# Masked softmax on one core: VectorE by half tiles, the first tile stored whole, and two later starts for GpSimd's narrow loads

## The chip, the core and the metric

The kernel runs on one core of a Trainium2 chip. The metric is device time in microseconds of one execution; smaller is better. Inputs and output lie in the chip's memory (HBM), and the kernel moves them through the core's on-chip memory (SBUF, 128 partitions).

## The reference

```python
def setup_inputs():
    batch, heads, seq_q, seq_k = 16, 8, 256, 256
    return {
        "x": np.random.randn(batch, heads, seq_q, seq_k).astype(np.float32),
        "lengths": np.random.randint(seq_k // 2, seq_k, size=batch).astype(np.int32),
    }

def reference(x, lengths):
    result = np.zeros_like(x)
    for b in range(batch):
        length = lengths[b]
        masked = x[b, :, :, :length].copy()
        masked = masked - np.max(masked, axis=-1, keepdims=True)
        exp_masked = np.exp(masked)
        result[b, :, :, :length] = exp_masked / np.sum(exp_masked, axis=-1, keepdims=True)
    return result
```

Each of the 16 batches has a length of its own between 128 and 255: a softmax over the first `length` of 256 columns, zeros behind them. The lengths of this draw are 188, 233, 229, 243, 195, 252, 165, 210, 222, 180, 209, 157, 159, 199, 214 and 248.

## The kernel before

One batch is one tile: 2048 rows of 256 numbers, as 128 partitions of 16 rows, 16 KB in each partition and 2 MB in all. SBUF holds eight such slots (`xt`), and the tile at position n lies in slot n % 8. Positions 0 to 2 are batches 1 to 3, position 3 is batch 0, and from 4 on position and batch agree (`batch_of`). In the text "tile n", "load n", "mask n" go by position, and "a" and "b" are the first and second eight rows of each partition (the halves).

Each tile goes through five steps, on four engines that run by themselves and wait for each other by semaphores only:

- **Load.** SyncE issues the loads of tiles 0 (two halves), 1 and 2 in full width at the start (L136, L138). GpSimd issues those of tiles 3 to 15 (`pick`, L158): it reads the batch's length and branches to a load of the smallest fitting width from a list, so that fewer bytes are read. The columns right of 160 in slots 3 to 7 have been zeroed before (L180). The first narrow load (tile 3) waits until the first half of tile 0 has been exponentiated (`s_exp` 1, L183), the second (tile 4) until two halves have been divided (`s_out` 2, L186). In the loop, each further load waits for the load two before it to have landed (L192, L196) and for its slot's last tile to have been stored (L193).
- **Mask**, on VectorE (`clip`, L234): in columns 128 to 255 it takes the minimum of x and a steep ramp that is very large left of `length` and very negative from there on, so that the exponential gives zero. Tile 0 by halves, all others whole. It counts `s_min`.
- **Exponential**, on ScalarE (L341): sixteen activations per tile, eight per half, each of which also sums its row. After each half it counts `s_exp`. The loop waits for the mask of the tile (`s_min` i // 2 + 2).
- **Divide**, on VectorE: reciprocal of eight sums (L255) and a product over one half (L258). It counts `s_out`, two per tile.
- **Store.** SyncE issues all stores on one queue (L147), in the order of the tiles: tile 0 in two halves, 1 to 7 as a half and two quarters, 8 to 12 and 15 in halves, 13 and 14 whole (`parts`). Each waits for its divide (L144), and the first one of a tile for the store of the tile two before it to have landed (L146). Ahead of the first store SyncE waits for three masks (`s_min` 3, L140), which is when the mask of tile 1 is done.

VectorE's order is written out by hand (L265 to L277): both half masks of tile 0, then for each tile divide a, the whole mask of the next tile, divide b; for tile 1 the mask of tile 2 comes ahead of both divides. After the last tile VectorE and TensorE look whether any sum was out of bounds, and a slower second pass, not taken with these inputs, would then run.

SyncE's transfers run on queue q1 of the profile, GpSimd's on q0. Both feed the same 16 transfer engines.

Of the kernel before, what the change touches and what calls it, by code (L numbers as in the profile page):

```python
# [16 lines left out]
ACT = mybir.EngineType.Activation  # L17
# [4 lines left out]
def kernel(  # L22
# [6 lines left out]
    nc = tc.nc  # L29
    P = nc.NUM_PARTITIONS  # L30

    batch, heads, seq_q, seq_k = x.shape
    rows = heads * seq_q
    assert rows % P == 0
    nt = rows // P
    half = nt // 2
# [8 lines left out]
    ahead = 3  # L45
# [11 lines left out]
    def parts(b):  # L57


        if b == 0:  # L60
            cuts = [0, half, nt]
        elif b < 8:
            cuts = [0, half, half + quarter, nt]
        elif b < 13 or b == batch - 1:
            cuts = [0, half, nt]
        else:
            cuts = [0, nt]
        return [slice(i, j) for i, j in zip(cuts, cuts[1:])]
# [30 lines left out]
    with tc.tile_critical(no_gpsimd_drain=True):  # L99
# [11 lines left out]
        s_min = sem("s_min")  # L111
        s_exp = sem("s_exp")
        s_out = sem("s_out")
# [10 lines left out]
        def length(engine, at):  # L124

            return nc.values_load(
                at,
                engines=[engine],
                skip_runtime_bounds_check_because="compared with constants, never an address",
            )  # L130
# [6 lines left out]
        for b in range(1, ahead):  # L137
            nc.sync.dma_start(out=xt[:, b], in_=x_f[batch_of(b)]).then_inc(s_ld[b + 1], 16)  # L138

        nc.sync.wait_ge(s_min, 3)  # L140
        for b in range(batch):
            s_b = s_st[b % 2]
            for s in parts(b):
                nc.sync.wait_ge(s_out, 2 * b + (s.stop - 1) // half + 1)  # L144
                if b >= 2 and s.start == 0:
                    nc.sync.wait_ge(s_b, 64 * (b // 2 + 1))  # L146
                nc.sync.dma_start(  # L147
                    out=out_f[batch_of(b), :, s, :], in_=xt[:, b % slots, s, :]
                ).then_inc(s_b, 16 * ((s.stop - s.start) // quarter))
# [1 line left out]

        def pick(v, b, slot, par, ws):

            if len(ws) == 1:
                w = ws[0]
                nc.gpsimd.dma_start(  # L158
                    out=xt[:, slot, :, :w], in_=x_n[:, b, :, :w]
                ).then_inc(s_sw[par], 16)  # L160
                return
            m = (len(ws) - 1) // 2
            with nc.gpsimd.If(v <= ws[m]):  # L163
                pick(v, b, slot, par, ws[: m + 1])
            with nc.gpsimd.Else():
                pick(v, b, slot, par, ws[m + 1 :])

        x_n = x_f.rearrange("b p t c -> p b t c")
        x_g = x_f.rearrange("b p t c -> p b (t c)")
# [10 lines left out]
            nc.gpsimd.memset(xt[:, b, :, low:], 0.0).then_inc(s_fill, 1)  # L180
        nc.gpsimd.wait_ge(s_word, 16)
        nc.gpsimd.wait_ge(s_fill, slots - ahead)
        nc.gpsimd.wait_ge(s_exp, 1)  # L183
        v_len = length(POOL, word[0:1, 0:1])
        pick(v_len, 0, ahead, 1, [160, 176, 192, 208, 224, seq_k])
        nc.gpsimd.wait_ge(s_out, 2)  # L186
        with nc.Fori(0, batch // 2 - 2, 1, engines=[POOL]) as q:
            for par in range(2):
                n = 2 * q + (ahead + 1 + par)
                v_len = length(POOL, word[0:1, bass.ds(2 * n, 1)])  # L190
                with nc.gpsimd.If(q >= 1):
                    nc.gpsimd.wait_ge(s_sw[par], 16 * q + 16 * par)  # L192
                    nc.gpsimd.wait_ge(s_st[par], 64 * q)  # L193
                if par:
                    with nc.gpsimd.Else():
                        nc.gpsimd.wait_ge(s_sw[par], 16)  # L196
                pick(v_len, bass.ds(n, 1), bass.ds(n % slots, 1), par, widths + [seq_k])
# [9 lines left out]
        v = 0  # L207

        def step(ins):
            nonlocal v  # L210
            v += 1
            ins.then_inc(s_v, 1)
# [18 lines left out]
        def clip(b, s, lo, hi):  # L231

            t = xt[:, b % slots, s, lo:hi]
            return nc.vector.scalar_tensor_tensor(  # L234
                out=t,
                in0=down[:, None, lo:hi].to_broadcast([P, s.stop - s.start, hi - lo]),
                scalar=len_s[:, batch_of(b) : batch_of(b) + 1],
                in1=t,
                op0=ALU.add,
                op1=ALU.min,  # L240
            )

        def mask(b, s):
            if b == 0:
                nc.vector.wait_ge(s_ld[s.start // half], 16)
            elif b < ahead:
                nc.vector.wait_ge(s_ld[b + 1], 16)
            else:
                nc.vector.wait_ge(s_sw[b % 2], 16 * ((b - 1) // 2))
            clip(b, s, mid, seq_k).then_inc(s_min, 1)  # L250

        def divide(b, h):
            s = slice(h * half, (h + 1) * half)
            nc.vector.wait_ge(s_exp, 2 * b + h + 1)
            step(nc.vector.reciprocal(out=inv_sum[:, b, s], in_=row_sum[:, b, s]))  # L255
            nc.vector.wait_ge(s_v, v)
            t = xt[:, b % slots, s, :]
            nc.vector.tensor_tensor(  # L258
                out=t,
                in0=t,  # L260
                in1=inv_sum[:, b, s, None].to_broadcast([P, half, seq_k]),
                op=ALU.mult,
            ).then_inc(s_out, 1)

        mask(0, slice(0, half))  # L265
        mask(0, slice(half, nt))
        for b in range(batch):


            first = b != 1  # L270
            if first:
                divide(b, 0)
            if b + 1 < batch:
                mask(b + 1, slice(0, nt))
            if not first:
                divide(b, 0)
            divide(b, 1)  # L277

# [56 lines left out]
        def rows(at, i):  # L337

            for j in range(half):
                e = x_h[:, at, j, :]  # L340
                ins = nc.scalar.activation(out=e, in_=e, func=EXP, accum_out=sum_h[:, i, j])  # L341
            ins.then_inc(s_exp, 1)


        nc.scalar.wait_ge(s_min, 1)
        rows(slice(0, 1), slice(0, 1))
        with nc.Fori(1, 2 * batch, 1, engines=[ACT]) as i:  # L347
            nc.scalar.wait_ge(s_min, i // 2 + 2)
            rows(bass.ds(i % (2 * slots), 1), bass.ds(i, 1))

        nc.scalar.wait_ge(s_redo, 1)
# [53 lines left out]
```

## Time and profile before

| | |
|---|---|
| median of 3 runs | 155.42 us (155.26 to 155.69) |
| the profiled execution | 155.72 us, its span 154.1 us |
| bytes moved | 61.57 MB (HBM read 27.98, written 33.55) |
| VectorE busy | 116.9 us (76%) |
| ScalarE busy | 105.3 us (68%) |
| GpSimd busy | 21.5 us (14%) |
| q1 (SyncE): bytes, share of the 16 engines | 39.85 MB, 62.6% |
| q0 (GpSimd): bytes, share | 21.69 MB, 35.4% |
| half divide (L258) | 2292 ns, 32 times |
| whole mask (L234), half mask | 2.35 us, 1.28 us |

The profile shows one execution. Its span begins and ends inside that execution, so the time of the run is 1.6 us longer. The page cuts the span into 40 slices of 3.85 us and gives for each the busy tenths of an engine, the mean busy share of the 16 transfer engines, and the GB/s that they moved. A row of a timeline has start, duration, engine, line and operation, and in brackets the idle time ahead of it and what ended that.

### The profile page before, as it was taken

What the parts mean: (1) busy time and instruction counts of PE and PEld (TensorE: products, weight loads), DVE (VectorE), ACT (ScalarE), POOL (GpSimd) and SP (SyncE); (2) the same over time, 40 slices, a digit from 0 to 9 for tenths busy, and PEclk for the clock granted to TensorE, in tenths of its full rate; (3) what the DMA queues carried; (4) which work ended last, traced back from release to release, by engine and by line L of the source; (5) the groups of instructions that cost most, each with busy time, mean ns of one, the idle gap of its engine ahead of it and who ended that gap; (6) DMA issues with size and microseconds to landing.
All of it is one profiled execution on the core that took longest, in us unless ns stands there. A gap on an engine that the chain in (4) does not pass through costs nothing.

```text
span 154.1 us, 1305 instructions
## 1 busy us (share of the span) xinstructions
PE 0.3 (0%) x2; PEld 0.2 (0%) x2; DVE 116.9 (76%) x91; ACT 105.3 (68%) x514; POOL 21.5 (14%) x28
## 2 busy tenths in 40 slices
PE   0000000000000000000000000000000000000000
PEld 0000000000000000000000000000000000000000
DVE  1349899969889696969697896969696566977800
ACT  3096899587795959595968859595959609688000
POOL 4953020100220200202020020202010000000000
DMA  4999999999999999999999999999999999999992
GB/s 115 421 451 417 327 372 417 419 409 441 417 401 391 418 416 422 405 414 418 395 426 406 413 412 404 415 420 414 419 420 413 432 437 413 430 442 430 425 419 106
DMA packets 10357, 61.57 MB, mean 400 GB/s; under 512 B 866, under 2 KB 978, under 8 KB 6642
## 3 DMA queue, kind: packets, MB, share of 16 engines
q1 hardware_dynamic: 5904, 39.85, 62.6%
q0 software_dynamic: 4448, 21.69, 35.4%
q14 instruction: 3, 0.02, 0.0%
q10 hardware_dynamic: 2, 0.00, 0.0%
HBM read 27.98 MB, written 33.55 MB: 399 GB/s over the span
## 4 chain that ended last, share of the span: by engine, by line
DMA 67%; DVE 16%; ACT 4%; issue 4%; SPq 2%; ACTq 1%; POOLq 0%; PE 0%
DMA out_dram<-xt 34%; DMA xt<-in_x_dram 33%; DVE xt L258 9%; DVE xt L234 6%; ACT xt L341 4%; SPq L147 1%; ACTq L341 1%; DVE inv_sum L255 1%; SPq L136 1%; DVE ends L290 0%; SPq L138 0%; POOLq L163 0%; POOLq L158 0%; DVE bad L293 0%; ACTq L347 0%
## 5 line engine op out<-in xcount | busy, mean ns | idle before, releaser
L341 ACT ACTIVATE xt<-xt (+1 forms) x256 | 102.4, 400 | 35.1 <-DVE xt L234 35.1
L258 DVE TENSOR_TENSOR xt<-xt,inv_sum 128x2048 f32<-128x2048 f32 x32 | 73.3, 2292 | 1.1
L341 ACT ACTIVATION_READ_ACCUMULATOR xt<-xt (+1 forms) x256 | 47.7, 186 | 0.0
L234 DVE SCALAR_TENSOR_TENSOR xt<-down,len_s,xt 128x2048 f32<-128x2048 f32 (+1 forms) x17 | 37.8, 2221 | 8.8 <-DMA xt<-in_x_dram 8.7
L158 POOL DMA_DIRECT2D xt<-in_x_dram x13 | 13.9, 1070 | 91.2 <-DMA out_dram<-xt 53.9
L255 DVE RECIPROCAL inv_sum<-row_sum 128x8 f32<-128x8 f32 x32 | 6.3, 198 | 16.6 <-ACT xt L341 16.6
L180 POOL MEMSET xt<- 128x1536 f32 x5 | 6.7, 1392 | 1.1 <-DVE len_s L225 1.1
L334 ACT ACT_TABLE_LOAD x1 | 1.3, 1283 | 1.6 <-SPq L99 1.6
L217 DVE TENSOR_SCALAR down<-iota_i 128x256 f32<-128x256 int32 x1 | 0.3, 300 | 1.6 <-POOL iota_i L171 1.6
L290 DVE TENSOR_REDUCE ends<-row_sum 128x1 f32<-128x256 f32 x2 | 0.7, 410 | 0.0
L204 PE MATMUL count<-bad,ones_c 128*1 128x3 bf16 x1 | 0.2, 165 | 142.9 <-DVE bad L293 142.9
L222 DVE CAST len_b<-word 1x16 bf16<-1x16 int32 x1 | 0.2, 163 | 0.4 <-DMA word<-in_lengths_dram 0.4
L225 DVE TENSOR_SCALAR len_s<-len_f 128x16 f32<-128x16 f32 x1 | 0.2, 175 | 0.3 <-PE len_f L202 0.3
L171 POOL IOTA iota_i<- 128x256 int32 x1 | 0.3, 332 | 0.6 <-SPq L99 0.6
L301 DVE TENSOR_REDUCE redo<-count 1x1 f32<-1x3 f32 x1 | 0.1, 149 | 0.3 <-PE count L204 0.3
L293 DVE TENSOR_SCALAR bad<-ends 128x1 bf16<-128x1 f32 x3 | 0.3, 150 | 0.0
L177 POOL MEMSET seed<- 1x1 f32 x2 | 0.2, 226 | 0.0
L204 PEld LDWEIGHTS count<-bad,ones_c 128*1 128x1 bf16 x1 | 0.1, 79 | 143.0 <-DVE bad L293 143.0
L334 ACT ACTIVATE warm<-const-float32-0.0 128x1 f32<-128x1 f32 x1 | 0.2, 203 | 0.0
L174 POOL MEMSET ones<- 1x128 bf16 x1 | 0.2, 194 | 0.0
L202 PE MATMUL len_f<-len_b,ones 1*128 1x16 bf16 x1 | 0.2, 164 | 2.6 <-DVE len_b L222 2.6
L290 DVE TENSOR_REDUCE ends<-len_s 128x1 f32<-128x16 f32 x1 | 0.2, 158 | 0.0
(7 smaller groups left out, 0.6 us busy)
## 6 DMA issues: line engine op xcount, KB each, us to landing
out_dram<-xt SPq DMA_DIRECT2D x21, 1024.0 KB
out_dram<-xt SPq DMA_DIRECT2D x14, 512.0 KB
xt<-in_x_dram POOLq DMA_DIRECT2D x3, 1728.0 KB, 16.6
xt<-in_x_dram SPq DMA_DIRECT2D x2, 2048.0 KB, 14.0
xt<-in_x_dram POOLq DMA_DIRECT2D x2, 2048.0 KB, 15.7
out_dram<-xt SPq DMA_DIRECT2D x2, 2048.0 KB
xt<-in_x_dram POOLq DMA_DIRECT2D x2, 1600.0 KB, 16.2
xt<-in_x_dram POOLq DMA_DIRECT2D x2, 1280.0 KB, 14.3
```

Of the source, the lines that this page charges most:

```text
L136: nc.sync.dma_start(out=xt[:, 0, s], in_=x_f[batch_of(0), :, s]).then_inc(s_ld[h], 16)
L147: nc.sync.dma_start(out=out_f[batch_of(b), :, s, :], in_=xt[:, b % slots, s, :]).then_inc(s_b, 16 * ((s.stop - s.start) // quarter))
L158: nc.gpsimd.dma_start(out=xt[:, slot, :, :w], in_=x_n[:, b, :, :w]).then_inc(s_sw[par], 16)
L171: nc.gpsimd.iota(iota_i, pattern=[[1, seq_k]], base=0, channel_multiplier=0).then_inc(s_iota, 1)
L180: nc.gpsimd.memset(xt[:, b, :, low:], 0.0).then_inc(s_fill, 1)
L204: nc.tensor.matmul(count, lhsT=ones_c, rhs=bad, start=True, stop=True).then_inc(s_count, 1)
L234: return nc.vector.scalar_tensor_tensor(out=t, in0=down[:, None, lo:hi].to_broadcast([P, s.stop - s.start, hi - lo]), scalar=len_s[:, batc ...
L255: step(nc.vector.reciprocal(out=inv_sum[:, b, s], in_=row_sum[:, b, s]))
L258: nc.vector.tensor_tensor(out=t, in0=t, in1=inv_sum[:, b, s, None].to_broadcast([P, half, seq_k]), op=ALU.mult,).then_inc(s_out, 1)
L290: step(nc.vector.tensor_reduce(out=ends[:, k : k + 1], in_=values, op=op, axis=AX))
L334: nc.scalar.activation(out=warm, in_=nc.const_aps.tensor(0.0, (P, 1), F32), func=EXP)
L341: ins = nc.scalar.activation(out=e, in_=e, func=EXP, accum_out=sum_h[:, i, j])
```

## The change

Six edits go together:

- VectorE's order becomes one loop over half tiles: divide of the half two before, then the mask of the current half. Every mask is now a half mask.
- ScalarE's loop waits for the mask of its own half (`s_min` i + 1).
- Tile 0 is stored whole, in one transfer, when both halves are divided.
- SyncE no longer waits for three masks ahead of the first store.
- GpSimd's first narrow load no longer waits for the first half's exponentials. The length is read and the branches are taken early, and the load itself waits for two divides (`s_out` 2), which also release the store of tile 0.
- GpSimd's second narrow load waits for three divides instead of two.

```diff
         if b == 0:
-            cuts = [0, half, nt]
+            cuts = [0, nt]
...
-        nc.sync.wait_ge(s_min, 3)
         for b in range(batch):
...
-        def pick(v, b, slot, par, ws):
+        def pick(v, b, slot, par, ws, gate=0):
 
             if len(ws) == 1:
                 w = ws[0]
+                if gate:
+                    nc.gpsimd.wait_ge(s_out, gate)
                 nc.gpsimd.dma_start(
                     out=xt[:, slot, :, :w], in_=x_n[:, b, :, :w]
                 ).then_inc(s_sw[par], 16)
                 return
...
-        nc.gpsimd.wait_ge(s_exp, 1)
         v_len = length(POOL, word[0:1, 0:1])
-        pick(v_len, 0, ahead, 1, [160, 176, 192, 208, 224, seq_k])
-        nc.gpsimd.wait_ge(s_out, 2)
+        pick(v_len, 0, ahead, 1, [160, 176, 192, 208, 224, seq_k], 2)
+        nc.gpsimd.wait_ge(s_out, 3)
...
-        mask(0, slice(0, half))
-        mask(0, slice(half, nt))
-        for b in range(batch):
-
-
-            first = b != 1
-            if first:
-                divide(b, 0)
-            if b + 1 < batch:
-                mask(b + 1, slice(0, nt))
-            if not first:
-                divide(b, 0)
-            divide(b, 1)
+
+        for i in range(2 * batch + 2):
+            if i >= 2:
+                divide((i - 2) // 2, i % 2)
+            if i < 2 * batch:
+                mask(i // 2, slice(i % 2 * half, (i % 2 + 1) * half))
...
-        nc.scalar.wait_ge(s_min, 1)
-        rows(slice(0, 1), slice(0, 1))
-        with nc.Fori(1, 2 * batch, 1, engines=[ACT]) as i:
-            nc.scalar.wait_ge(s_min, i // 2 + 2)
+        with nc.Fori(0, 2 * batch, 1, engines=[ACT]) as i:
+            nc.scalar.wait_ge(s_min, i + 1)
             rows(bass.ds(i % (2 * slots), 1), bass.ds(i, 1))
```

More of the change, by code (lines that the diff above doesn't have):

```diff
@@ L163, in pick @@
             with nc.gpsimd.If(v <= ws[m]):
-                pick(v, b, slot, par, ws[: m + 1])
+                pick(v, b, slot, par, ws[: m + 1], gate)
             with nc.gpsimd.Else():
-                pick(v, b, slot, par, ws[m + 1 :])
+                pick(v, b, slot, par, ws[m + 1 :], gate)
         x_n = x_f.rearrange("b p t c -> p b t c")
```

## The prediction

> **What bounds the kernel now.** I read the slices of the span first, then single microseconds around the one dip, the DMA queues in the same stretches, the engines' timelines at both ends, and the waits.
>
> ```profile
> DMA  4999999999999999999999999999999999999992
> GB/s 115 421 451 417 327 372 417 419 409 441 417 401 391 418 416 422 405 414 418 395 426 406 413 412 404 415 420 414 419 420 413 432 437 413 430 442 430 425 419 106
> ```
>
> The transfer engines are full in every slice but the first and the last: 61.57 MB move at some 415 GB/s, and neither VectorE (76%) nor ScalarE (68%) is full. So the time is a start, bytes over rate, and an end; a change counts only by what it does to the rate, to gaps, and to the end. The one dip is in slices 5 and 6. In single microseconds (columns: stretch, length, busy time of PE, PEld, DVE, ACT, POOL, clock, DMA share, GB/s):
>
> ```profile
> 16.00:17.00 1.00, 0.00 (x0) 0.00 (x0) 0.97 (x2) 0.84 (x5) 0.00 (x0) 1.00 1.03 428
> 17.00:18.00 1.00, 0.00 (x0) 0.00 (x0) 1.00 (x1) 1.00 (x6) 0.00 (x0) 1.00 0.86 273
> 18.00:19.00 1.00, 0.00 (x0) 0.00 (x0) 0.34 (x1) 1.00 (x7) 0.00 (x0) 1.00 0.90 235
> 19.00:20.00 1.00, 0.00 (x0) 0.00 (x0) 0.94 (x1) 1.00 (x6) 0.00 (x0) 1.00 0.92 258
> 20.00:21.00 1.00, 0.00 (x0) 0.00 (x0) 1.00 (x1) 1.00 (x7) 0.03 (x1) 1.00 1.02 342
> 21.00:22.00 1.00, 0.00 (x0) 0.00 (x0) 0.97 (x3) 1.00 (x6) 1.00 (x1) 1.00 1.04 435
> ```
>
> The missing bytes against 426 GB/s are 153+191+168+84 = 596 KB, or 1.40 us. Who moves bytes there (q0 is GpSimd's queue, q1 SyncE's; packets, MB, share), from 16.9 to 17.0, 18.8 to 20.3, 20.3 to 20.5 and 16.9 to 21.9:
>
> ```profile
> q0 software_dynamic: 4, 0.02, 44.5%
> ...
> q0 software_dynamic: 85, 0.39, 94.1%
> ...
> q1 hardware_dynamic: 3, 0.02, 29.0%
> ...
> q0 software_dynamic: 200, 0.92, 62.9%
> ```
>
> So q1's loads are through by about 18.0, its first store moves nothing before 20.4, and until then the first narrow load runs alone, at 260 GB/s. The issues that belong to it:
>
> ```profile
> 12.38 1.29 POOL L158 DMA_DIRECT2D xt<-in_x_dram  x1 [2.67 <-issue]
> ...
> 38.34 1.16 POOL L158 DMA_DIRECT2D xt<-in_x_dram  x1 [8.16 <-issue]
> ...
> 15.93 0.42 SPq L147 DMA_DIRECT2D out_dram<-xt  x1
> ```
>
> GpSimd's load needs 4.5 us from issue to first packet (12.38 to 16.9; again 38.34 to about 42.95, where q0 had run empty). The first store needs the same 4.5 us (15.93 to 20.4), though the very first load needs only 1.04 us (issue 1.13, bytes from 2.17). At the other end:
>
> ```profile
> 124.57 2.35 DVE L234 SCALAR_TENSOR_TENSOR xt<-down,len_s,xt 128x2048 f32<-128x2048 f32 x1 [3.14 <-DMA xt<-in_x_dram]
> ...
> 130.51 0.20 DVE L255 RECIPROCAL inv_sum<-row_sum 128x8 f32<-128x8 f32 x1 [1.15 <-ACT xt L341]
> ...
> 142.08 0.20 DVE L255 RECIPROCAL inv_sum<-row_sum 128x8 f32<-128x8 f32 x1 [0.66 <-ACT xt L341]
> 142.32 2.29 DVE L258 TENSOR_TENSOR xt<-xt,inv_sum 128x2048 f32<-128x2048 f32 x1
> ...
> 144.64 0.36 SPq L147 DMA_DIRECT2D out_dram<-xt  x1
> ```
>
> VectorE waits for load 14 until 124.57 and from there needs 20.04 us to the last divide. The last store, issued at 144.64, moves its 1 MB only in the last 2.5 us before the bytes end near 151.4, from 148.9: it stands 4.3 us behind other stores. That is all the slack the chain load 14, VectorE, last store has, issue latency included.
>
> **The change, part by part.** *Half tiles on VectorE.* The 15 masks of 2.35 us become 30 of 1.28 us (the two rows of the first tile): 3.2 us more busy time, beside a full DMA, so free until the end. There it changes the chain. A half mask hands over after 1.20 us (1.28 less the 0.08 by which rows overlap), reciprocal and divide after 2.44 us (21.33 to 23.77); from a mask's end to the reciprocal that needs its exponentials are 3.59 us (126.92 to 130.51). From the start S of mask 14's first half: divide 13b starts at S+1.20, mask 14b 3.64, divide 14a 4.87, mask 15a 7.31, divide 14b 8.51, mask 15b 10.95, divide 15a 12.18, divide 15b 15.82 (waits for ScalarE), done S+18.34. That is 1.7 us shorter than today. Load 15 must be there by S+7.3; today it lands about 7 us after load 14. ScalarE's loop waits for s_min i+1, one half each, at no cost.
>
> *The start.* Mask 1a starts at 13.55 as today's whole mask does, hands over at 14.75, and divide 0b ends at 17.27 (0.23 + 2.29) against 18.34 today; the second half's exponentials are done by 14.1. SyncE's wait for the third mask goes, but the first tile now goes as one 2 MB store at about 17.3, where its first half was issued at 15.93. Behind that wait on SyncE stand only later stores. The loads on q1, without company, end at about 17.9. GpSimd's load moves from 12.38 to about 17.4: the length is read and the branches are taken before the wait, so nothing follows it but the issue. Its first packet then comes at 17.4+4.5 = 21.9. Queued behind it on GpSimd is only the second narrow load, which now waits for divide 1a (14.75+3.64 = 18.4, done 20.9) plus 2.6 us of register work (18.34 to 20.97): 23.5. It is in the queue long before the first has landed, so that wait is free; were it not, q0 would stand empty.
>
> What is unknown is when the first store's bytes start: 1.04 us after issue (18.4) by the first load's row, 4.5 us (21.8) by today's first store. The trace leaves a third reading: 1.7 us after the loads' last completion at 18.7, which gives 20.2 here. I take 20.2, between the ends, since both observed stretches fit it. The DMA then idles 2.2 us (0.4 to 3.8) and gets back the 1.40 us of the dip: +0.8 us (−1.0 to +2.4). In a sentence of its own: the Trainium skill, page "DMA: Bandwidth & Descriptors", section "Latency and other measured facts", gives about 0.6 us to the first byte of a transfer from SyncE and about 1 us from GpSimd; by it the gap would nearly vanish, and the trace's two GpSimd rows of 4.5 us disagree with it.
>
> *The narrow loads fall behind.* q0 has work without a break from 16.9 to the end of load 15, near 131, since each load waits for the second one before it (L192): what it loses at the start it can't win back while stores run beside it. By 21.9 it has moved 0.92 MB today and nothing after the change. Then come the bigger packets of the whole-tile store: the queues take turns packet by packet (149 each from 108 to 112 us), and 16 KB against 8 KB per turn halves the load's turns. Of tile 0 about 1.37 MB are left at 21.9, 84 turns where there were 168, so 84 x 4608 B = 0.39 MB less. Together 1.31 MB (1.10 to 1.51 by the store's start). From 42 to 131 us q0 moved 16.40 MB, 0.184 MB/us: load 14 lands 7.1 us later (6.0 to 8.2). Stores running dry early on (tile 2's second divide now stands behind mask 3a, which waits for load 3) give back up to 2 us. I take 7.0 (4 to 8.2).
>
> *The end.* S = 124.57+7.0 = 131.6; last divide 149.9; last store issued 149.95. The stores, meanwhile, are ahead by what the loads lack, so at 4.9 us a tile (428 GB/s from 131.5 to 151) they run dry while VectorE gives a tile each 7.3 us: the last store stands behind little. Its latency lies between 1.04 and 4.5 us; I take 2.0, nearer the first load, as no load is ahead of it. Bytes 151.95 to 154.45, against 151.4 today: **+3.05 us**. The DMA account of the start (+0.8) is a floor below this and isn't added. By the bounds: S+18.34+0.05+1.04+2.5 with 4.0 gives 150.5, where the floor decides, and 8.2 with 4.5 gives 158.2, +6.8.
>
> The profiled execution took 155.72 us (span 154.1 and 1.62 around it), 0.30 above the median 155.42. 155.72+3.05 = 158.8, put to the median 158.5.
>
> **The rivals.** *Both queues start at once, and it is faster.* If store and load move bytes 1.04 us after issue, both run from 18.4. The dip goes and 0.4 us of idle stay: −1.0. Loads lose 0.6 MB by 21.9 and 0.18 MB to the big packets: 4.2 us, so S = 128.8, last divide 147.1, store bytes 148.2 to 150.7: −0.7 us, 154.7. The very first load speaks for it, both GpSimd rows against it. The Trainium skill's two figures above are this case, on another ground. 0.14.
>
> *The store starts as late as today.* With 4.5 us the DMA idles 3.8 us (17.9 to 21.8 with nothing moving), loads are 8.2 us late, S = 132.8, and the end is +4.2 (latency 2.0) to +6.8: 159.6 to 162.2. For it is that this is the same store on the same queue; against it that its 4.5 us may be the load ahead. 0.20.
>
> *The loads catch up.* If gaps between stores let q0 win back 3 us or more, the end stays hidden and the start alone counts: +0.8, 156.2 (same within a tenth where the gap is 1.4 us). For it: q0 alone moves 260 GB/s against some 150 beside 8 KB packets. Against it: SyncE waits 98 us for landings, so stores are seldom out. 0.18, of it 0.04 without a measurable change.
>
> **How the numbers follow.** The forecast (157.3 to 159.5) has 0.45, and 0.03 is left for others. About 0.3%, 0.47 us, is what a measurement of this kernel can tell. Slower: 0.45+0.20+0.14+0.02 = 0.81; same 0.04+0.01 = 0.05; faster 0.14. The range 155.2 to 161.8 leaves out the faster rival and the upper tip of the late store.
>
> **What would show it.** Right: a stretch of 1 to 4 us without bytes near 18 to 21; first packets of q0 near 21.9; mask 14a starting 4 to 8 us after 124.57; DMA slices below 9 between 140 and 150; VectorE's last divide near 150. Wrong: store and load bytes from 18.5 on, or load 14 within 3 us of today. Then the end stays hidden and the time is 154.5 to 156.5.

## The result and the profile after

The changed kernel takes 159.33 us (median of 6 runs, 158.66 to 160.04) against 155.45 us: a ratio of 1.0244 (95% interval 1.0214 to 1.0275). The profiled execution took 159.47 us, its span 157.7 us instead of 154.1. Bytes are the same; their mean rate fell from 400 to 390 GB/s. The slices of the page show where:

```profile
DMA  4999897999999999999999999999999999993994
GB/s 112 438 430 441 374 332 264 410 414 419 431 417 421 385 411 409 418 409 414 418 401 423 409 418 415 412 411 419 414 418 416 423 417 445 393 407 141 465 397 202
```

There are two holes now. The dip at the start, in slices 5 and 6 before, is in slices 5 to 7 and deeper, and slice 37 has lost most of its bytes. Larger stretches (columns: stretch, length, busy time of PE, PEld, DVE, ACT, POOL, clock, DMA share, GB/s), first of the kernel before:

```profile
17.00:28.00 11.00, 0.00 (x0) 0.00 (x0) 10.18 (x8) 11.00 (x56) 1.15 (x1) 1.00 0.98 367
...
131.00:151.00 20.00, 0.17 (x1) 0.08 (x1) 12.85 (x15) 9.16 (x46) 0.00 (x0) 1.00 1.01 428
```

and of the changed one:

```profile
17.00:28.00 11.00, 0.00 (x0) 0.00 (x0) 10.90 (x10) 9.97 (x49) 2.45 (x2) 1.00 0.93 316
...
131.00:151.00 20.00, 0.00 (x0) 0.00 (x0) 15.74 (x14) 13.21 (x64) 0.00 (x0) 1.00 0.87 367
```

The start lacks (367-316) x 11 = 561 KB against the kernel before, which is 1.3 us at 426 GB/s. The end lacks (428-367) x 20 = 1.2 MB. Between them, from 28 to 131 us, the mean rates are 415 before and 414 after. The end hole in the timeline of VectorE, where load 14 is waited for, and on SyncE:

```profile
133.99 1.28 DVE L234 SCALAR_TENSOR_TENSOR xt<-down,len_s,xt 128x1024 f32<-128x1024 f32 x1 [4.34 <-DMA xt<-in_x_dram]
...
142.73 2.29 DVE L258 TENSOR_TENSOR xt<-xt,inv_sum 128x2048 f32<-128x2048 f32 x1
...
150.03 2.29 DVE L258 TENSOR_TENSOR xt<-xt,inv_sum 128x2048 f32<-128x2048 f32 x1
...
145.05 0.37 SPq L146 DMA_DIRECT2D out_dram<-xt  x1
...
152.35 0.37 SPq L146 DMA_DIRECT2D out_dram<-xt  x1
```

Mask 14 starts at 133.99 instead of 124.57. Divide 14b is done at 145.02, and its store is issued at once. From 143.8 to 145.8 the engines start nothing but two completions; then the last 4.2 MB, from 145.88 on, run without a break to the end. At the start, GpSimd's issues:

```profile
17.72 1.30 POOL L159 DMA_DIRECT2D xt<-in_x_dram  x1 [8.01 <-DVE xt L258]
23.93 1.15 POOL L159 DMA_DIRECT2D xt<-in_x_dram  x1 [4.92 <-issue]
```

and the queues (packets, MB, share; a packet counts where it starts, so a short stretch can have over 100%) from 18.0 to 18.4, 18.4 to 24.2, 24.2 to 24.4 and 23.9 to 26.3:

```profile
q1 hardware_dynamic: 18, 0.25, 144.8%
...
q1 hardware_dynamic: 113, 1.85, 97.7%
...
q0 software_dynamic: 2, 0.01, 11.1%
...
q0 software_dynamic: 129, 0.59, 79.1%
```

The store of tile 0, issued at 17.43, moves bytes from about 18.3. The first load gets its first packet only at about 24.3, when that store is nearly through; the store of tile 1's first half, issued at 21.11, then waits until 26.3 while q0 is alone.

The store of tile 0 has the engines to itself from 18.4 to 24.2, and they are busy (97.7%), yet it moves only 1.85 MB there, 319 GB/s. Up to q0's first packet the mean is:

```profile
17.00:24.30 7.30, 0.00 (x0) 0.00 (x0) 7.23 (x7) 6.60 (x33) 1.66 (x2) 1.00 0.91 310
```

Against 426 GB/s that is 0.85 MB less, of the 1.21 MB that are missing from 17 to 28: most of the loss at the start lies ahead of q0's first packet.

### The profile page after: what moved, and what is told of

Same layout as the page of the kernel before. It is cut to its first block, busy times and chain, and to the rows that moved or that the text cites. A ratio compares the mean times of both kernels' runs of the same rounds, so it can differ in the third digit from the quotient of the medians.

```text
span 157.7 us, 1330 instructions
## 1 busy us (share of the span) xinstructions
PE 0.3 (0%) x2; PEld 0.2 (0%) x2; DVE 118.9 (75%) x106; ACT 107.1 (68%) x514; POOL 21.5 (14%) x28
## 4 chain that ended last, share of the span: by engine, by line
DMA 69%; DVE 17%; issue 6%; ACT 3%; POOLq 2%; ACTq 1%; PE 0%; SPq 0%; DVEq 0%
DMA xt<-in_x_dram 69%; DVE xt L258 10%; DVE xt L234 5%; ACT xt L334 3%; DVE inv_sum L255 1%; POOLq L126 1%; ACTq L334 1%; POOLq L164 1%; POOLq L159 1%; DVE ends L283 0%; DVE bad L286 0%; POOLq L191 0%; PE count L204 0%; POOLq L193 0%; DVE redo L294 0%
## 5 line engine op out<-in xcount | busy, mean ns | idle before, releaser
L334 ACT ACTIVATE xt<-xt x256 | 102.7, 402 | 41.0 <-DVE xt L234 41.0
L234 DVE SCALAR_TENSOR_TENSOR xt<-down,len_s,xt 128x1024 f32<-128x1024 f32 x32 | 41.0, 1280 | 28.8 <-DMA xt<-in_x_dram 28.7
L334 ACT ACTIVATION_READ_ACCUMULATOR xt<-xt x256 | 47.8, 187 | 0.0
```

The lines of the kernel that those rows point to most:

```text
L234: return nc.vector.scalar_tensor_tensor(out=t, in0=down[:, None, lo:hi].to_broadcast([P, s.stop - s.start, hi - lo]), scalar=len_s[:, batc ...
```

## The experiments

The theory is the prediction's: the late first load puts all loads behind, load 14 comes late, and the end then waits for VectorE. The rivals are the half masks, the whole-tile store, and a loss in the start alone.

| kernel | time, us | ratio to before (95%) | mask 14 starts, us | last divide ends, us | GB/s from 17 to 28 us |
|---|---|---|---|---|---|
| before | 155.45 | 1 | 124.57 | 144.61 | 367 |
| changed | 159.33 | 1.0244 (1.0214-1.0275) | 133.99 | 152.32 | 316 |
| e1 changed, first load early | 155.80 | 1.0018 (1.0002-1.0033) | 125.48 | 143.82 | 358 |
| e2 before, both waits | 157.13 | 1.0127 (1.0066-1.0187) | 129.90 | 149.94 | 322 |
| e3 before, half tiles | 155.86 | 1.0026 (1.0014-1.0038) | 127.94 | 146.33 | 366 |
| e4 changed, tile 0 in halves | 159.11 | 1.0248 (1.0213-1.0283) | 133.03 | 151.37 | 311 |
| e5 changed, load 3 at one divide | 156.38 | 1.0046 (1.0029-1.0063) | 125.60 | 143.94 | 357 |
| e6 changed, load 4 at two divides | 157.97 | 1.0157 (1.0142-1.0173) | 131.94 | 150.27 | 297 |
| e7 changed, quarters to tile 12 | 157.75 | 1.0141 (1.0126-1.0157) | 127.00 | 145.34 | 313 |
| e8 before, load 3 sooner | 155.45 | 0.9989 (0.9979-0.9999) | 124.48 | 144.52 | 369 |
| e9 before, load 3 in full rows | 156.07 | 1.0036 (1.0024-1.0048) | 123.66 | 143.69 | 392 |
| e10 before, no mask wait | 155.85 | 1.0023 (1.0005-1.0041) | 125.73 | 145.77 | 368 |
| e11 before, tile 0 whole | 155.57 | 0.9999 (0.9987-1.0010) | 123.84 | 143.89 | 377 |

Each ratio is taken against runs of the kernel before on the same chip.

**e1, the first load early again.**

```diff
+        nc.gpsimd.wait_ge(s_exp, 1)
         v_len = length(POOL, word[0:1, 0:1])
-        pick(v_len, 0, ahead, 1, [160, 176, 192, 208, 224, seq_k], 2)
+        pick(v_len, 0, ahead, 1, [160, 176, 192, 208, 224, seq_k])
```

> The changed kernel with one part undone: the first narrow load again starts after the first half's exponentials, everything else stays changed. Theory (the late loads set the end): the mask of tile 14 starts within 2 us of 124.57 instead of 133.99, and the time falls to 155.0 to 156.8; the dip behind the first loads may last longer than before, since the store of tile 0 comes at 17.4. Rival (half masks and the whole-tile store cost the time): 158 to 159.5, whatever load 14 does.

```profile
125.48 1.28 DVE L235 SCALAR_TENSOR_TENSOR xt<-down,len_s,xt 128x1024 f32<-128x1024 f32 x1 [4.35 <-DMA xt<-in_x_dram]
```

Mask 14 starts at 125.48 and the time is 155.80: of the 2.4% only 0.2% are left with half masks, whole-tile store and the second wait still in place. Without the late first load the loss is all but gone, so the theory's first step holds and the rival falls. By itself this run doesn't say which of the two holes costs the time, since both nearly go (358 GB/s from 17 to 28, 426 from 131 to 151); e7 separates them. The dip is longer than in the kernel before, as expected: q0 is alone from 17.7 to 22.1.

**e2, GpSimd's two waits alone.** From the kernel before; the `gate` argument of `pick` comes with them.

```diff
-        nc.gpsimd.wait_ge(s_exp, 1)
         v_len = length(POOL, word[0:1, 0:1])
-        pick(v_len, 0, ahead, 1, [160, 176, 192, 208, 224, seq_k])
-        nc.gpsimd.wait_ge(s_out, 2)
+        pick(v_len, 0, ahead, 1, [160, 176, 192, 208, 224, seq_k], 2)
+        nc.gpsimd.wait_ge(s_out, 3)
```

> The kernel before with only the two new waits of GpSimd: first narrow load at two divides, second at three; whole masks, tile 0 in two halves, SyncE's wait kept. Theory: load 14 comes 6 to 9.5 us late, and as the chain from it to the last divide is 20.0 us here instead of 18.3, the time is 158.5 to 161.5, not below the changed kernel. Rival: 155 to 156, the waits being hidden behind full transfers.

157.13 us lies between the two spans: the waits do cost, but less than the theory said. Load 14 is 5.3 us late, not 6 to 9.5. The first load, issued at 18.94, has its first packet at 22.9, 4.0 us later, although stores of tile 0 are on q1 until 23.6. The start has lost as much as in the changed kernel (322 GB/s), the end less:

```profile
131.00:151.00 20.00, 0.00 (x0) 0.00 (x0) 16.81 (x18) 12.99 (x64) 0.00 (x0) 1.00 0.93 395
```

So the waits alone aren't the 2.4%; some 4 us of load 14's delay come only when the other edits stand beside them.

**e3, half tiles alone.** From the kernel before; ScalarE's first half, which stood ahead of its loop, goes into the loop.

```diff
-        (the order of before, lines 265 to 277)
+        for i in range(2 * batch + 2):
+            if i >= 2:
+                divide((i - 2) // 2, i % 2)
+            if i < 2 * batch:
+                mask(i // 2, slice(i % 2 * half, (i % 2 + 1) * half))
...
-            nc.scalar.wait_ge(s_min, i // 2 + 2)
+            nc.scalar.wait_ge(s_min, i + 1)
```

> The kernel before with only the half tiles on VectorE and ScalarE's wait that belongs to them. SyncE's wait for three masks is met by three half masks here, about 1 us earlier than before. Theory: the 3 us more of VectorE work lie beside full transfers: 154.8 to 155.8. Rival (VectorE's longer work is the cost): 157.5 to 159.

155.86 is just above the theory's span and far below the rival's. The trace shows something that I hadn't counted: load 14 is 3.4 us late here too. Load 3 is issued at 12.88 instead of 12.38. The third half mask lets SyncE issue the first store at 15.16 instead of 15.93, and q0 is alone for a shorter time (86 packets from 17.6 to 19.7 instead of 135 from 17.6 to 20.4). Load 5, released by load 3, is issued at 31.07 instead of 29.62. That is 1.4 us; load 8 is issued 3.0 us late (55.32 against 52.30), and why the lag grows on the way is open (e10 has load 5 as late, and load 14 only 1.2 us late). The end absorbs it: the last divide comes 1.7 us later, within the 4.3 us by which the last store of the kernel before stands behind others. In the changed kernel half tiles and waits come together, and it has 9.4 us where e2 has 5.3 and e3 3.4; with the first load early, e1, half tiles leave only 0.9.

**e4, tile 0 in two transfers.** From the changed kernel.

```diff
-            cuts = [0, nt]
+            cuts = [0, half, nt]
...
-                nc.sync.wait_ge(s_out, 2 * b + (s.stop - 1) // half + 1)
+                nc.sync.wait_ge(s_out, max(2, 2 * b + (s.stop - 1) // half + 1))
```

> The changed kernel, but tile 0 goes out in two transfers of 1 MB, both released by the second divide like the one of 2 MB. By the prediction's term for big packets, load 14 comes about 2 us earlier (131.5 to 132.5 instead of 133.99) and the time is 157 to 158. If instead the first narrow load simply gets no turn until what is ahead of it has gone, whatever its packets, load 14 and the time stay within 0.7 us of the changed kernel (158.6 to 160).

159.11, and q0's first packet comes at 24.3 as in the changed kernel. Mask 14 moves by 0.96 us, between the two readings (1.5 to 2.5, and up to 0.7); the packet size of that store is at most a small part of what delays the loads.

**e5, a smaller dose.** From the changed kernel; the first load is then issued at 13.98.

```diff
-        pick(v_len, 0, ahead, 1, [160, 176, 192, 208, 224, seq_k], 2)
+        pick(v_len, 0, ahead, 1, [160, 176, 192, 208, 224, seq_k], 1)
```

> The changed kernel with a smaller dose: the first narrow load waits for one divide instead of two (issue about 14.0 instead of 17.7). Theory (the later the first load, the later load 14, and only what exceeds some 4 us of slack costs time): mask 14 starts between 126 and 130, time 155.5 to 157.3. Rival (any wait on the divides costs the whole amount): 158.5 to 159.5.

156.38, within the theory's span; load 14 is even earlier than it said (125.60), so what is left, 0.8 us, isn't load 14's. The start shows 0.3 us of it (357 against 367 GB/s, q0 alone from 17.4 to 21.7); the place of the rest wasn't found.

**e6, the second load at two divides.** From the changed kernel.

```diff
-        nc.gpsimd.wait_ge(s_out, 3)
+        nc.gpsimd.wait_ge(s_out, 2)
         with nc.Fori(0, batch // 2 - 2, 1, engines=[POOL]) as q:
```

> The changed kernel with the second narrow load at two divides again instead of three. The prediction took that wait to be free, as the load only queues behind the first: 158.6 to 160.0, load 14 within 0.7 us of 133.99. Rival (the second wait holds q0 up): load 14 over 1 us earlier, 157 to 158.4.

The rival was right: 157.97, and load 14 is 2.05 us earlier. The second wait isn't free. Load 3 lands only 0.2 us earlier than in the changed kernel; the difference grows on the way to load 14. What the runs show at the place itself is that q0 moves 193 packets instead of 129 before tile 1's store gets a turn. Why more packets are ready for q0 when load 4 is issued earlier is not settled.

**e7, smaller stores late in the run.** From the changed kernel.

```diff
-        elif b < 8:
+        elif b < 13:
             cuts = [0, half, half + quarter, nt]
-        elif b < 13 or b == batch - 1:
+        elif b == batch - 1:
             cuts = [0, half, nt]
```

> The changed kernel, but tiles 8 to 12 are stored like 1 to 7, in a half and two quarters (4 KB packets), so that the loads get more bytes per turn late in the run; the start is untouched. Theory (the time hangs on when load 14 lands, wherever the delay arose): load 14 comes 1.5 to 4 us earlier, the time is 156.5 to 158.3. Rival (the lost time lies in the start and is not to be had back): 158.8 to 160.

This edit touches nothing before the store of tile 8, yet load 14 comes 7 us earlier and 1.6 us of the 3.9 are back. From 94 to 133 us q0 moves, in the changed kernel and then in e7:

```profile
q0 software_dynamic: 1413, 6.07, 38.9%
```

```profile
q0 software_dynamic: 1536, 7.91, 50.0%
```

For each byte that q1 moves the loads get more, the end is full again (425 GB/s from 131 to 151), and what remains is the start:

```profile
131.00:151.00 20.00, 0.17 (x1) 0.08 (x1) 14.26 (x18) 10.74 (x53) 0.00 (x0) 1.00 1.01 425
...
17.00:28.00 11.00, 0.00 (x0) 0.00 (x0) 10.90 (x10) 9.97 (x50) 2.44 (x2) 1.00 0.93 313
```

(367-313) x 11 = 594 KB, or 1.4 us, of a span that is 2.0 us longer than before. So the change has two prices: about 2.2 us that remain when load 14 is only 2.4 us late (127.00, within the slack), 1.4 of them visible in the start, and 1.6 us more because load 14 is 9.4 us late. The smaller stores weren't run in the kernel before, so what they cost or save there is not known.

**e8, load 3 sooner.** From the kernel before; the load is issued at 11.19, not at the 10 that I took.

```diff
         nc.gpsimd.wait_ge(s_fill, slots - ahead)
-        nc.gpsimd.wait_ge(s_exp, 1)
```

> The kernel before, with the first narrow load issued as soon as the lengths and the zeroed columns are there (about 10 instead of 12.4), opposite to the change. If the dip at 17 to 20.4 comes only from q0 being alone there, an earlier q0 runs beside the loads of tiles 1 and 2 and the dip gets shorter: 153.9 to 154.9. If the first store on q1 has to wait for packets of q0 that the engines already hold, the dip stays about as long: 155.1 to 155.9.

155.45, on the rival's side: the dip stays (201 GB/s from 18 to 19), and q1's first store starts at 20.2 instead of 20.4.

**e9, load 3 in full rows.** From the kernel before; 0.5 MB more are read.

```diff
-        pick(v_len, 0, ahead, 1, [160, 176, 192, 208, 224, seq_k])
+        pick(v_len, 0, ahead, 1, [seq_k])
```

> The kernel before, but the load of tile 3 always takes full rows (2 MB in 16 KB packets instead of 1.5 MB in pieces of 768 B). It measures what makes the stretch slow in which q0 is alone. If short pieces are slow when nothing runs beside them, the rate from 18 to 20 rises from 250 to 400 GB/s or more; the 0.5 MB more (1.2 us) and the 1.4 us of the dip then cancel: 154.8 to 156.2. If q0 is slow there for another reason, the rate stays below 300 GB/s and the time is 156.3 to 157.5.

156.07 lies in the first reading's span, the rate between the two (442 and 328 GB/s in the two microseconds from 18 to 20). The missing bytes from 17 to 28 go from 649 to 374 KB. But with bigger packets q0 takes turns from q1's loads, which now run until 19.9, so q0 is hardly alone and the run doesn't show that short pieces alone are slow. That q0 is alone doesn't fix its rate either: e11, with the same narrow load, has 335 GB/s from 18 to 22.

**e10, no wait for masks.** From the kernel before; the first store is issued at 13.64.

```diff
-        nc.sync.wait_ge(s_min, 3)
         for b in range(batch):
```

> The kernel before without SyncE's wait for three masks: the store of the first half of tile 0 is issued at about 13.5 instead of 15.9, while the loads are still running. If its packets then stand directly behind the loads, the dip goes (154.0 to 154.9), with load 14 a little later (below 4 us, inside the slack). If its start still depends on how many packets of q0 the engines hold, 155.2 to 156.2.

155.85: the dip stays. Here q1 is never without packets for long, and yet the rates from 16 to 19 are low:

```profile
16.00:17.00 1.00, 0.00 (x0) 0.00 (x0) 0.97 (x3) 0.67 (x3) 0.00 (x0) 1.00 1.07 295
17.00:18.00 1.00, 0.00 (x0) 0.00 (x0) 1.00 (x1) 1.00 (x7) 0.00 (x0) 1.00 1.28 273
18.00:19.00 1.00, 0.00 (x0) 0.00 (x0) 0.51 (x1) 1.00 (x6) 0.00 (x0) 1.00 0.37 86
```

So it isn't only q0's being alone: in every run the whole DMA is slow for 3 us or more around q0's first packets, whichever queue has packets.

**e11, SyncE's two edits alone.** From the kernel before.

```diff
-            cuts = [0, half, nt]
+            cuts = [0, nt]
...
-        nc.sync.wait_ge(s_min, 3)
```

> The kernel before with only the two edits on SyncE: no wait for three masks, tile 0 stored whole (issue at 18.4). The first narrow load starts early as before. Theory: q0 is alone from 17.6 until the store gets its turn, some 1 to 2 us longer than before, so the dip costs 0.3 to 1.0 us more; load 14 isn't late: 155.6 to 156.6. Rival (the whole-tile store is what delays the loads): load 14 over 3 us late and 157 to 159.

155.57, no change, 0.03 below the span that I gave; load 14 isn't late at all. By itself the whole-tile store costs nothing. In the changed kernel the load is issued 0.3 us after it and has its first packet when it is nearly through; e4 shows the same with two transfers, so it is the place of this store that goes with the late load, not its size.

None of these kernels beats the one before by more than 0.2%.

## Why the prediction was right, point by point

**The outcome.** 158.5 was forecast and 159.33 measured. The sign, the path (late first load, late load 14, an end that waits for VectorE) and the range were right. That the number is so near is in part luck, since errors of opposite sign cancel: load 14 came 2.4 us later than the sum has it, the last store's latency was 0.97 us (152.35 to 153.32) instead of 2.0, and the kernel before has a tail of 0.05 MB after the 151.4 that the sum counts from, with packets starting until 152.2. Of the forecast's signs of being right the hole late in the run came as written; the stretch without bytes at the start was under 1 us, and the first packet of q0, mask 14 and the last divide came 1.4 to 2.5 us later than the signs had them.

**The chain at the end was right to 0.01 us.** From mask 14's start to the last divide 18.34 us were worked out and 18.33 measured (133.99 to 152.32). That some delay is absorbed is borne out by e3. That the stores run dry happened one store earlier than the forecast said: the gap is ahead of tile 14's store, which waits for divide 14b (S+11.03: 145.02), and the last three transfers then run back to back to the same end.

**The delay of load 14 was too small: 7.0, bounds 4 to 8.2, measured 9.4.** Three parts of that step failed. First, q0's first packet came at 24.3 and not at 21.9. From issue to first packet 3.4 to 4.8 us hold in nine of the kernels, and about 6.6 us were needed in the four (changed, e4, e6, e7) in which the load is issued 0.3 us after the store of tile 0; e2, with 4.0 us, shows that stores on q1 don't always cost that much. Second, the term for 84 turns of 16 KB packets was wrong in kind: q0 got no turn at all until that store had nearly gone, and e4 shows that its packet size matters little. The Trainium skill, page "DMA: Bandwidth & Descriptors", section "Queues, rings and completion order", has each engine take turns between its queues packet by packet. The trace agrees in the steady stretches (139 against 141 packets from 104 to 108 us). It shows no turns before a queue's first transfer: there the other queue moved between 86 packets (e3) and 312 (e11) in most runs, and at most about 20 in e9 and e10. Whether the waiting queue had its work ready by then no run shows. Third, a term was missing: a lag makes later loads meet the 8 KB stores of tiles 8 to 12 where they met quarters. GpSimd's issues of loads 12 and 14, each released by the load two before it, show the lag grow (where a row names a store, the slot's store was long done, tile 4's near 69 us before); first of the kernel before, then of the changed one:

```profile
89.05 1.15 POOL L158 DMA_DIRECT2D xt<-in_x_dram  x1 [7.89 <-DMA out_dram<-xt]
...
103.99 1.15 POOL L158 DMA_DIRECT2D xt<-in_x_dram  x1 [6.33 <-issue]
```

```profile
95.74 1.15 POOL L159 DMA_DIRECT2D xt<-in_x_dram  x1 [7.88 <-issue]
...
113.41 1.15 POOL L159 DMA_DIRECT2D xt<-in_x_dram  x1 [7.81 <-DMA out_dram<-xt]
```

The lag is 6.7 us at load 12 and 9.4 us at load 14. By the packets of the trace the store of tile 8 begins at 93.9 us instead of 97.5, and loads 11 and 12, which moved for 7.4 us each, move for 8.3 and 8.7. With quarters (e7) the lag is 6.8 us at load 14's issue.

**The start was +0.8 and measured +1.3 by missing bytes, out of the wrong parts.** The store began 0.84 us after its issue, so there is no idle gap of 2.2 us: no packet of data starts for 0.8 us (17.44 to 18.27). By the first-byte figure that I quoted from the Trainium skill (some 0.6 us on SyncE) the store was nearly right; 4.5 us, as in the kernel before, is what it took where GpSimd's load had been issued ahead of it (3.6 to 4.6 us in e1, e3, e5, e8, e9 and e11). But I let the dip's 1.40 us be won back. It wasn't: it moved to 20 to 27 and grew. E10 shows that a dip comes without q1's absence. Its cause is open: in the changed kernel 0.85 of the 1.21 MB are lost before q0's first packet, most of it while the store of tile 0 runs alone. The dip is about twice as large where q0 begins beside stores (the changed kernel, e2, e4, e6, e7: 297 to 322 GB/s) as where it begins at the end of the first loads (before, e1, e3, e5, e8, e10: 357 to 369). The forecast took the start for a floor of 0.8 us below the end's 3.05; e7 puts what remains without a late end at some 2.2 us, of which 1.4 are placed.

**"That wait is free" was wrong.** The second narrow load's third divide costs 0.9% (e6 against the changed kernel: 157.97 and 159.33).

**"Half tiles free until the end" holds** with 0.26% (e3), though they too put loads behind, in part by way of SyncE's wait for three masks, which the text didn't see. The rival of both queues starting at once had the store right and the load wrong; the late store and the loads that catch up didn't occur.

## What to carry to other kernels

Where transfers fill the span, look for the stream that nobody waits for yet: loads that run ahead in the background hold a lead. A later start of a few microseconds wasn't made up here while stores took their turns, and it was paid at the far end, where the last loads release a chain of compute. Price such a delay as delay minus slack, and look for bytes lost at the start besides: load 14 came 3.4 us late for 0.3% (e3, start as before), but 2.4 us late for 1.4% (e7) and 5.3 us for 1.3% (e2), both with a start as poor as the changed kernel's, and 9.4 us for 2.4%. And a lag can be repaired elsewhere: smaller packets on the rival queue gave the loads most of their lead back (e7).

## What the runs showed of the hardware that I had not expected

A queue's first transfer can start late when the other queue has begun to work. SyncE's first store moved bytes 0.84 us after its issue in the changed kernel, and 3.6 to 4.6 us after it in the seven (before, e1, e3, e5, e8, e9, e11) in which GpSimd's load had been issued 2 us or more ahead, in some of them in part behind q1's own loads. Between those loads and that store q0 moved 86 packets in e3 and 312 in e11, so the time from issue is steadier than the number of packets; what sets it is open. GpSimd's first load needed 6.6 us when it was issued 0.3 us after the store.

Around the first packets of GpSimd's queue 0.4 to 0.8 MB of transfers are missing where it begins at the end of the first loads, and 1.1 to 1.4 MB where it begins beside stores, against 426 GB/s from 17 to 28 us, wherever in time it was put. In the changed kernel 0.62 MB of that is missing from 18.4 to 24.2, while a single store has busy engines to itself at 319 GB/s. No run shows why.
